# The output projection of a decoder layer by Strassen's scheme, with its operands in the attention's memory

## The chip, the core and the metric

The kernel runs on one core of a Trainium2 chip. A core has TensorE (matrix products; PE in the profile), VectorE (DVE), ScalarE (ACT), GpSimd (POOL) and SyncE (SP, whose queue issues all transfers of this kernel). SBUF is the working memory, PSUM holds eight banks of 512 fp32 columns into which matmuls accumulate. The metric is the device time of one execution in microseconds.

## The reference

```python
h = rmsnorm(x, norm_pre_g)                      # x: (1, 2048, 1024) fp32
z = einsum('bsd,de->bse', h, w_in)              # 1024 -> 4096 columns
q, k, v, g_attn, c_h, c_b, c_c, g_conv = split(z)
# 12 heads of 64, rotary q and k, three dilated windows mixed by their softmax sums
attn_out = o.reshape(B, S, 768) * silu(g_attn)
conv_out = c_b * causal_depthwise_conv(c_c * c_h, conv_w) * silu(g_conv)   # 256 columns
mixed = concatenate([attn_out, conv_out], axis=-1)                         # 1024
y = einsum('bse,ed->bsd', mixed, w_out)         # 1024 x 1024
x = x + rmsnorm(y, norm_post_g)
```

## The kernel before, in words

Precision: an fp32 operand is stored as two parts, a cast to a shorter float (ScalarE) and the rest (VectorE, "split": operand minus cast). A product is three matmuls: high x high, high x low, low x high.

The input projection runs over 32 units of 512 tokens: groups 0 and 7 are the convolution's columns, 1 to 6 pairs of heads, four token chunks each. Normalised x is kept in DRAM as two parts and streamed in by `x_stream` (L472, nine buffers `xp_r`); input weights lie in eight buffers `wp_r`. The four banks of a unit are read by VectorE, for the convolution at L502, L503, L513 and L478. `attn_unit` follows with scores (L627, L655), transposed probabilities (L680), their split (L686) and the products with the values (L699). It keeps keys in `KK`, queries in `q_r` and `q1_r`, values in `v2_r` and `v1_r`, probabilities in `p4_r`, `p1_r` and `pt_r`. Gated results go to DRAM (`mix_d`: L807 from the attention, L523 from the convolution).

The output projection begins when the last product of the attention is done (`gate`). The attention's pool is closed and a new one holds `wo`, the gain `gpost` and other buffers. Sixteen pieces (128 rows x 512 columns) of `w_out` are loaded (L880), cast (L882) and split (L883). For each chunk of 512 tokens eight blocks of the mixed activations are loaded (L892), cast (L893) and split (L894). For each of its four token tiles (128 tokens, every fourth one) and each column half, 8 blocks x 3 matmuls accumulate into one bank (L908 to L910). Then ScalarE squares the bank with a sum over columns (L914), VectorE multiplies it with the gain (L919); the root of the mean square (L921 and the four small operations L382 to L385) scales it onto the residual (L928), and two stores follow (L930).

Order: no engine order is written by hand. Every operation is added to a `Plan` with its engine, an estimated duration, a priority (a lower number goes first) and the buffers that it reads and writes. A list scheduler gives each free engine the ready operation of lowest number; a buffer comes from a `Ring`, whose tokens are handed out in the order in which they were made unless the ring is unordered. The instructions are then issued in that order, and each engine and SP's queue execute theirs in order. URG is a large negative priority for what frees a bank.

Of the kernel before, what the change touches and what calls it, by code (L numbers as in the profile page):

```python
# [34 lines left out]
KT = D // 128  # L35
# [260 lines left out]
def hybrid_layer(ctx: ExitStack, tc: tile.TileContext, x, w_in, w_out, conv_w, g_pre, g_post,  # L296
# [25 lines left out]
    mix_d = [[dram.tile([128, C], F32, name=f"mix{e}_{b}") for b in range(NB)] for e in range(KT)]  # L322
# [26 lines left out]
    attn = ExitStack()  # L349
    ap_ = attn.enter_context(tc.tile_pool(name="attn", bufs=1))  # L350
# [5 lines left out]
    p4_r = ring(ap_, "p4", 2, [128, 4, C])  # L356
    p1_r = ring(ap_, "p1", 2, [128, 4, 256])
# [33 lines left out]
    W = {}  # L391

    def weights_in(grp, i):
# [8 lines left out]
        else:  # L402
# [6 lines left out]
        add("DVE", dvet(C) + 0.07, pc, lambda: vec.tensor_tensor(w.ap[:, 1], raw.ap, f(w.ap[:, 0]), op=ALU.subtract),  # L409
            r=[raw, (w, 0)], w=[(w, 1)], after=XL[i - 1:i] if grp == 0 and i else (), port=True)  # L410
# [58 lines left out]

    def x_stream(n, kt):  # L470
        s = XT[n, kt] = Tok(xp_r)
        add("DMA", dmat(512), n * 100 - 20 + kt, lambda: nc.sync.dma_start(f(s.ap), xt_d[n % NB][kt]), r=[("xt", n % NB, kt)], w=[s])  # L472
# [17 lines left out]
    U = {}  # L490

    def conv_unit(n, i, b, zs):
        pe, pr = URG + n * 100, n * 100 + 60
# [6 lines left out]
        t = table(b, pr - 100) if i else T[b]  # L500
# [22 lines left out]
        add("DMA", dmat(256), pr, lambda: nc.sync.dma_start(mix_d[6 + i][b], g.ap), r=[g], w=[("mix", 6 + i, b)])  # L523
# [5 lines left out]
    def attn_unit(n, p, b, zs):  # L529
# [196 lines left out]
        for i in range(0, len(groups), 2):  # L726
            visit = groups[i:i + 2]
            add("PE", sum(g[0] for g in visit), pr, lambda visit=visit: [g[1]() for g in visit], r=[k for g in visit for k in g[2]],
                w=[k for g in visit for k in g[3]], after=x_last, mode=1)
            for g in visit:  # L730
                g[4]()
# [75 lines left out]
        add("DMA", dmat(256), pr, lambda: nc.sync.dma_start(mix_d[p][b], gs.ap), r=[gs], w=[("mix", p, b)])  # L807

    attn_last = []
# [44 lines left out]
    OUT = {}  # L854
    or_r = uu_r + raw_r + rp_r + g_r

    def open_out():
        if OUT:
            return
        attn.close()  # L860
        op_ = ctx.enter_context(tc.tile_pool(name="outp", bufs=1))
        OUT["wo"] = [op_.tile([128, 2, D], F32R, name=f"wo{e}") for e in range(KT)]
        OUT["gpost"] = op_.tile([128, D], F32, name="gpost")
        for s, t in zip(xr_r, ring(op_, "xr", 2, [128, D])):
            s.ap = t.ap
        for s, t in zip(y_r, ring(op_, "y", 2, [128, D])):
            s.ap = t.ap
        for s, t in zip(mx_r, ring(op_, "mx", 2, [128, 2, C], F32R)):
            s.ap = t.ap
        for s, t in zip(ys_r, ring(op_, "ys", 4, [128, 8])):  # L870
            s.ap = t.ap

    xr_r, y_r, ys_r, mx_r = (Ring([Slot() for _ in range(k)]) for k in (2, 2, 4, 2))
    gate = add("DMA", 0.0, 3300, open_out, after=attn_last, w=["open"])
    add("DMA", dmat(512), 3301, lambda: nc.sync.dma_start(OUT["gpost"], g_post.to_broadcast([128, D])), w=["gpost"], after=[gate])
    for e in range(KT):
        for j in range(2):
            raw = Tok(or_r)
            dl = slice(j * C, (j + 1) * C)
            add("DMA", dmat(256), 3302 + e, lambda e=e, dl=dl, raw=raw: nc.sync.dma_start(raw.ap, w_out[e * 128:(e + 1) * 128, dl]),  # L880
                w=[raw], after=[gate])
            add("ACT", actt(C), 3302 + e, lambda e=e, dl=dl, raw=raw: act.copy(OUT["wo"][e][:, 0, dl], raw.ap), r=[raw], w=[("wo", e, j, 0)])  # L882
            add("DVE", dvet(C), 3302 + e, lambda e=e, dl=dl, raw=raw: vec.tensor_tensor(  # L883
                OUT["wo"][e][:, 1, dl], raw.ap, f(OUT["wo"][e][:, 0, dl]), op=ALU.subtract), r=[raw, ("wo", e, j, 0)], w=[("wo", e, j, 1)], port=True)

    ms_r = mx_r + wp_r
    for b in range(NB):
        MX = []
        for e in range(KT):
            pr = 3320 + 100 * b + e  # L890
            raw, m = Tok(or_r), Tok(ms_r)
            add("DMA", dmat(256), pr, lambda e=e, b=b, raw=raw: nc.sync.dma_start(raw.ap, mix_d[e][b]), r=[("mix", e, b)], w=[raw], after=[gate])  # L892
            add("ACT", actt(C), pr, lambda raw=raw, m=m: act.copy(m.ap[:, 0], raw.ap), r=[raw], w=[(m, 0)])  # L893
            add("DVE", dvet(C), pr, lambda raw=raw, m=m: vec.tensor_tensor(m.ap[:, 1], raw.ap, f(m.ap[:, 0]), op=ALU.subtract),  # L894
                r=[raw, (m, 0)], w=[(m, 1)], port=True)
            MX.append(m)
        for i in range(4):
            pr = 3400 + 100 * b + 20 * i
# [13 lines left out]
            for j in range(2):  # L912
# [3 lines left out]
                if j == 0:  # L916
                    add("DVE", 0.07, pr + URG, lambda sq=sq: vec.tensor_scalar(
                        sq.ap[:, 0:1], sq.ap[:, 4:5], 1.0 / D, EPS, op0=ALU.mult, op1=ALU.add), r=[(sq, 4)], w=[(sq, 0)])
# [58 lines left out]
```

## Time and profile before

| what | value |
|---|---|
| median of 3 runs | 1229.0 us (1225.31 to 1232.68) |
| the profiled execution | 1228.29 us, span of its instructions 1226.5 us |
| TensorE busy | 1213.1 us (99%), 6952 matmuls |
| VectorE busy | 842.0 us (69%) |
| ScalarE busy | 685.6 us (56%) |
| mean granted clock of TensorE | 0.998 |

The span runs from the first to the last instruction; the device time holds some 1.8 us more. Busy time of an engine is the time covered by its instructions; matmuls overlap, and a busy TensorE is not one at its peak. Line numbers are those of the kernel before.

### The profile page before, as it was taken

To read this page: it belongs to the slowest core of one execution; us is meant where nothing else is said; L and a number is where in the kernel's file an instruction comes from. 1 tells how busy PE (TensorE), PEld (TensorE's weight loads), DVE (VectorE), ACT (ScalarE), POOL (GpSimd) and SP (SyncE) were. 2 spreads that over 40 slices of the span, in tenths; PEclk is the share of its full clock that TensorE was granted. 3 is DMA by queue.
4 is the path that set the end of the run, shared out by engine and by line. 5 is a ranking of instruction groups with operands and counts; after the bars stand their busy time and mean duration, and the time that the engine had idled before them with its cause. 6 is when DMAs were issued, how large, how long until landed. Compare 5 with 4: busy or idle time off the path is not lost.

```text
span 1226.5 us, 20984 instructions
## 1 busy us (share of the span) xinstructions
PE 1213.1 (99%) x6952; PEld 1010.5 (82%) x6952; DVE 842.0 (69%) x2179; ACT 685.6 (56%) x1814; POOL 260.6 (21%) x212
## 2 busy tenths in 40 slices
PE   8999999999999999999999999999999999999997
PEld 7888888888878888888888888888888888888886
DVE  5565577877777778786778787787778656544343
ACT  6532546766656667667658666677667434223121
POOL 0011122323222332212323232322333111000000
PEclk9999999999999999999999999999999999999999
DMA  9979677766777666865877757765777759642331
GB/s 344 369 305 343 241 241 258 243 189 211 238 243 224 209 214 219 287 200 160 257 221 268 242 174 268 250 192 189 247 246 270 231 200 374 215 151 94 103 103 69
DMA packets 140573, 279.09 MB, mean 228 GB/s; under 512 B 31536, under 2 KB 73648, under 8 KB 140464
## 3 DMA queue, kind: packets, MB, share of 16 engines
q1 hardware_dynamic: 140464, 277.75, 68.1%
q8 instruction: 55, 0.90, 0.3%
q14 instruction: 54, 0.44, 0.1%
HBM read 214.05 MB, written 51.05 MB: 216 GB/s over the span
## 4 chain that ended last, share of the span: by engine, by line
PE 96%; DVE 1%; DMA 1%; SPq 0%; issue 0%; ACT 0%; DVEq 0%
PE z L844 18%; PE z L846 18%; PE z L845 17%; PE st L699 8%; PE st L680 8%; PE st L909 5%; PE st L908 5%; PE st L910 5%; PE st L627 4%; PE st L655 3%; PE st L844 1%; PE st L846 1%; PE st L845 1%; PE st L441 1%; PE st L590 1%; DMA rp<-rp 0%
## 5 line engine op out<-in xcount | busy, mean ns | idle before, releaser
L844 PE MATMUL z<-xt,w 128*128 128x512 f32 x960 | 397.2, 414 | 0.0
L846 PE MATMUL z<-xt,w 128*128 128x512 f32 x960 | 376.8, 392 | 0.0
L845 PE MATMUL z<-xt,w 128*128 128x512 f32 x960 | 375.4, 391 | 0.0
L846 PEld LDWEIGHTS z<-xt,w 128*128 128x128 f32 x960 | 180.2, 188 | 40.9
L844 PEld LDWEIGHTS z<-xt,w 128*128 128x128 f32 x960 | 180.9, 188 | 32.3 <-issue 3.8
L845 PEld LDWEIGHTS z<-xt,w 128*128 128x128 f32 x960 | 181.3, 189 | 25.8
L686 DVE TENSOR_TENSOR pt<-st,pt 128x512 fp32r<-128x512 f32 x216 | 142.2, 678 | 47.6 <-ACT pt L685 45.7
L638 ACT ACTIVATE p<-p,sm 128x128 f32<-128x128 f32 (+3 forms) x192 | 105.8, 554 | 73.5 <-DVE sm L634 73.1
L685 ACT CAST pt<-st 128x512 fp32r<-128x512 f32 x216 | 119.9, 579 | 36.1 <-PE st L680 34.2
L699 PEld LDWEIGHTS st<-pt,v 128*128 128x128 f32 x852 | 122.1, 190 | 16.8 <-DVE pt L686 4.3
L699 PE MATMUL st<-pt,v 128*128 128x256 f32 x852 | 132.6, 286 | 2.4 <-DVE pt L686 2.4
L680 PE MATMUL st<-cst,p 128*128 128x128 f32 x852 | 121.8, 273 | 0.0
L719 DVE TENSOR_TENSOR uu<-st,uu 64x256 f32<-64x256 f32 x192 | 80.2, 420 | 58.8 <-ACT uu L718 54.8
L748 POOL TENSOR_TENSOR uu<-uu 128x512 f32<-128x512 f32 x48 | 72.4, 1508 | 207.2 <-DVE uu L719 207.1
L680 PEld LDWEIGHTS st<-cst,p 128*128 128x128 f32 x852 | 100.2, 140 | 18.4 <-issue 3.0
L634 DVE CUSTOM_DVE_ANT_0 p<-st,cst 128x128 f32<-128x128 f32 (+3 forms) x192 | 81.8, 487 | 47.5 <-PE st L627 47.2
L717 ACT COPY uu<-st 64x256 f32<-64x256 f32 x192 | 70.2, 368 | 61.9 <-PE st L699 56.0
L666 ACT ACTIVATE p<-p,e 128x256 f32<-128x256 f32 (+1 forms) x192 | 94.7, 498 | 12.2 <-DVE e L662 12.1
L914 ACT ACTIVATE y<-st 128x512 f32<-128x512 f32 x32 | 19.2, 599 | 129.9 <-PE st L910 129.9
L558 POOL TENSOR_TENSOR rp<-rp,cs 128x512 f32<-128x512 f32 x24 | 36.2, 1510 | 228.1 <-DMA rp<-rp 109.0
L662 DVE CUSTOM_DVE_ANT_0 p<-st,cst 128x256 f32<-128x256 f32 (+1 forms) x192 | 66.9, 411 | 21.7 <-PE st L655 21.5
L909 PE MATMUL st<-wo,w 128*128 128x512 f32 x192 | 75.6, 394 | 0.0
(140 smaller groups left out, 1804.6 us busy)
## 6 DMA issues: line engine op xcount, KB each, us to landing
xt<-xt SPq DMA_DIRECT2D x256, 512.0 KB
cs<-t SPq DMA_DIRECT2D x28, 768.0 KB
raw<-in_w_in SPq DMA_DIRECT2D x59, 256.0 KB
rp<-rp SPq DMA_DIRECT2D x192, 64.0 KB
vd<-v SPq DMA_DIRECT2D x96, 128.0 KB
v<-vd SPq DMA_DIRECT2D x24, 512.0 KB
ab<-ad SPq DMA_DIRECT2D x48, 256.0 KB
mix<-g SPq DMA_DIRECT2D x32, 256.0 KB
```

What stands on the lines that cost most here:

```text
L634: add("DVE", dvet(w) + 0.01, pr + URG, lambda h=h, r=r, P4=P4: vec.tensor_tensor_reduce(P4.ap[:, r, 0:w], ps[h].ap[:, (r - r0) * w:(r - r0 ...
L638: add("ACT", actt(w) + 0.19, pr, lambda h=h, r=r, P4=P4: act.activation(P4.ap[:, r, 0:w], P4.ap[:, r, 0:w], AF.Exp, bias=s4(0, h)[:, r:r + ...
L666: add("ACT", actt(256 - lo[g]) + 0.19, pr, lambda h=h, g=g, P1=P1: act.activation(P1.ap[:, g, lo[g]:], P1.ap[:, g, lo[g]:], AF.Exp, bias=E ...
L680: nc.tensor.transpose(ps.ap[:, i * 128:(i + 1) * 128], pp.ap[:, a, c * 128:(c + 1) * 128], ident)
L685: add("ACT", actt(m * 128, True), pr + URG, lambda: act.copy(pt.ap[:, :m, 0, :], p4()), r=[ps], w=[(pt, 0)])
L686: add("DVE", dvet(m * 128), pr + URG, lambda: vec.tensor_tensor(pt.ap[:, :m, 1, :], p4(), f(pt.ap[:, :m, 0, :]), op=ALU.subtract), r=[ps, ...
L699: mm(dst, v, pt.ap[:, i], start=s, stop=e)
L719: add("DVE", dvet(256), pr + URG, lambda: vec.tensor_tensor(cols(a, lo), o()[lo:lo + 64, 0], cols(a, lo), op=ALU.add), r=[O], w=[(a, (h, h ...
L844: mm(z.ap, w.ap[:, 0, js], xt.ap[:, 0], start=kt == 0, stop=False)
L845: mm(z.ap, w.ap[:, 0, js], xt.ap[:, 1], start=False, stop=False)
L846: mm(z.ap, w.ap[:, 1, js], xt.ap[:, 0], start=False, stop=kt == KT - 1)
L909: mm(z.ap, m.ap[:, 0, il], wo[:, 1, dl], start=False, stop=False)
```

## The change

The output projection is done for pairs of token tiles (`q`, eight pairs) as a 2 x 2 block product: rows are the two tiles, the summed index is halved (blocks 0 to 3 and 4 to 7), the columns are the two halves of 512. Winograd's form of Strassen's scheme needs seven block products of 4 blocks x 3 matmuls each: A11 B11, S3 T3, S2 T2, A22 T4, S1 T1, A12 B21, S4 B22, in this order, with four sums of activations (S) and four of weights (T). The sums run on VectorE in fp32 before the cast and split, so there are 28 weight forms (seven for each of four blocks) and seven forms per pair. Three products accumulate onto a bank that already holds another product and has been copied before.

The attention's buffers stay allocated. Weight forms lie in `KK`, the queries', values' and probabilities' buffers; those of `p4_r` and `p1_r` are closed and reopened for six more. Five forms, (B21, 3) and (B22, 0 to 3), lie in input weight buffers and are loaded again (`late`). Token forms use the nine x buffers and three input weight buffers. Two gates open the homes: keys and queries after the last scores, the rest after the last product of the attention. The mixed activations are stored per chunk as (block, row, token) and loaded for four blocks and one tile at a time. Residual loads are halved in size.

```diff
-    mix_d = [[dram.tile([128, C], F32, name=f"mix{e}_{b}") for b in range(NB)] for e in range(KT)]
+    mix_d = [dram.tile([KT, 128, C], F32, name=f"mix{b}") for b in range(NB)]
...
+    FORMS = ("B11", "T3", "T2", "T4", "T1", "B21", "B22")
...
+    wo_r = Ring(early + later + anew[0] + anew[1], False)
+    gates = [gated(early, score_last + w_last, lambda: None), gated(later + anew[0], attn_last + w_last, lambda: layout(0))]
+    home = len(wo_r)
+    ys_r = ring(cp, "ys", 4, [128, 8])
+    wr_r = uu_r + raw_r + list(g_r)[2:]
+    mr_r = uu_r + list(g_r)[2:]
+    or_r = rp_r + g_r
+    wl_r = Ring(list(wp_r)[:4 * len(FORMS) - home], False)
+    ms_r = Ring(list(xp_r) + list(wp_r)[4 * len(FORMS) - home:])
...
+    def part(name, e, t, pr):
+        form = WF[name, e]
+        add("ACT", actt(C), pr, lambda: act.copy(form.ap[:, 0], t.ap), r=[t], w=[(form, 0)])
+        return add("DVE", dvet(C), pr, lambda: vec.tensor_tensor(form.ap[:, 1], t.ap, f(form.ap[:, 0]), op=ALU.subtract),
+                   r=[t, (form, 0)], w=[(form, 1)], port=True)
...
+        def at(name, e=e):
+            return 3303 + 8 * e if e < 2 else 3319 + 2 * FORMS.index(name) + 0.1 * e
...
+        part("B11", e, r11, at("B11"))
+        less("T3", r11, r12, r11)
+        less("T3", r12, r22, r12)
+        part("T3", e, r12, at("T3"))
+        less("T2", r12, r22, r11)
+        part("T2", e, r12, at("T2"))
+        less("T4", r12, r21, r12)
+        part("T4", e, r12, at("T4"))
+        part("T1", e, r11, at("T1"))
...
+        def mixed(half, i):
+            t = Tok(mr_r)
+            x_ops.append(add("DMA", dmat(256), po - 90 + 4 * i + half, lambda b=b, i=2 * h + i: nc.sync.dma_start(
+                cells(t), mix_d[b][4 * half:4 * half + 4, :, 128 * i:128 * i + 128].rearrange("e p t -> p e t")),
+                r=[("mix", 4 * half + k, b) for k in range(4)], w=[t], after=loads[7:8] + streams[-1:]))
+            return t
...
+        a11, a21, a22, a12 = mixed(0, 0), mixed(0, 1), mixed(1, 1), mixed(1, 0)
+        form("A11", a11)
+        sums("S3", a21, a11, a21, ALU.subtract)
+        form("S3", a21)
+        sums("S2", a21, a22, a21, ALU.subtract)
+        form("S2", a21)
+        form("A22", a22)
+        sums("S1", a22, a21, a11, ALU.add)
+        form("S1", a22)
+        form("A12", a12)
+        sums("S4", a12, a12, a21, ALU.subtract)
+        form("S4", a12)
...
+        def keep(bank):
+            y = Tok(or_r)
+            add("ACT", actt(C, True), po + URG, lambda: act.copy(y.ap, bank.ap), r=[bank], w=[y])
+            return y
+        def plus(bank, y):
+            add("DVE", dvet(C), po + URG, lambda: vec.tensor_tensor(y.ap, bank.ap, y.ap, op=ALU.add), r=[bank], w=[y])
...
+        product(0, B[0], "A11", "B11", True)
+        c11 = keep(B[0])
+        product(1, B[1], "S3", "T3", True)
+        c22 = keep(B[1])
+        product(2, B[0], "S2", "T2", False)
+        c21 = keep(B[0])
+        product(3, B[1], "A22", "T4", False)
+        plus(B[1], c21)
+        finish(2 * h + 1, 0, c21, c21, lower)
+        product(4, B[0], "S1", "T1", False)
+        plus(B[0], c22)
+        finish(2 * h + 1, 1, c22, c22, lower)
+        store(2 * h + 1, (c21, c22), lower)
+        product(5, B[2], "A12", "B21", True)
+        plus(B[2], c11)
+        finish(2 * h, 0, c11, c11, upper)
+        product(6, B[0], "S4", "B22", False)
+        c12 = Tok(or_r)
+        finish(2 * h, 1, B[0], c12, upper)
+        store(2 * h, (c11, c12), upper)
```

`product` adds twelve matmuls of 128 x 512 as before; `finish` squares and multiplies with the gain, `store` does the root, the residual and the two stores.

## Rows read from the trace of the kernel before

**Rows 1.** The page: span, busy time of each engine (share of the span, instructions), and the chain of work that ended last.

```profile
span 1226.5 us, 20984 instructions
...
PE 1213.1 (99%) x6952; PEld 1010.5 (82%) x6952; DVE 842.0 (69%) x2179; ACT 685.6 (56%) x1814; POOL 260.6 (21%) x212
...
PE 96%; DVE 1%; DMA 1%; SPq 0%; issue 0%; ACT 0%; DVEq 0%
```

**Rows 2.** The three longest groups of waits of TensorE over the whole span: engine and line that waited, for whom, us in total, times, longest.

```profile
PE st L441 <- DMA p<-in_x: 2.7, 4, 1.1
PE st L699 <- DVE pt L686: 2.4, 1, 2.4
PE st L817 <- DVE u L497: 1.1, 1, 1.1
```

**Rows 3.** The timeline of TensorE around the first and the last matmul of the output projection: start, us of one, engine, line, operation, output<-inputs.

```profile
1041.15 0.39 PE L846 MATMUL st<-xt,w 128*128 128x512 f32 x1
...
1043.87 0.39 PE L846 MATMUL st<-xt,w 128*128 128x512 f32 x1
1044.09 0.39 PE L908 MATMUL st<-wo,mx 128*128 128x512 f32 x1
...
1219.32 0.39 PE L910 MATMUL st<-wo,mx 128*128 128x512 f32 x1
```

**Rows 4.** TensorE's groups of one of the projection's three lines from 1044 us to the end: count, busy us, mean ns of one, idle us before (the other two lines, L908 and L910, have the same two counts).

```profile
L909 PE MATMUL st<-wo,w 128*128 128x512 f32 x192 | 75.6, 394 | 0.0
...
L909 PE MATMUL st<-wo,mx 128*128 128x512 f32 x64 | 24.9, 389 | 0.0
```

**Rows 5.** Busy time of each engine in the stage of the output projection: us and instructions, TensorE's granted clock, DMA share, GB/s.

```profile
1044.09:1219.50 175.41, 175.41 (x769) 144.02 (x767) 77.00 (x188) 42.40 (x104) 2.77 (x2) 1.00 0.37 122
```

**Rows 6.** The timeline of VectorE: the first split of an output weight, neighbouring splits, the last one, the first read of an input projection's bank in the last unit, and the end of the first token tile.

```profile
1007.12 0.68 DVE L883 TENSOR_TENSOR wo<-raw,wo 128x512 fp32r<-128x512 f32 x1
...
1031.31 0.68 DVE L883 TENSOR_TENSOR wo<-rp,wo 128x512 fp32r<-128x512 f32 x1
1031.91 0.68 DVE L883 TENSOR_TENSOR wo<-uu,wo 128x512 fp32r<-128x512 f32 x1
...
1037.33 0.68 DVE L883 TENSOR_TENSOR wo<-rp,wo 128x512 fp32r<-128x512 f32 x1
...
1042.25 0.69 DVE L502 TENSOR_TENSOR rp<-z,cs 128x512 f32<-128x512 f32 x1 [1.84 <-PE z L846]
...
1057.66 0.16 DVE L382 RECIPROCAL ys<-ys 128x1 f32<-128x1 f32 x1 [0.80 <-ACT ys L921]
...
1058.49 1.41 DVE L928 SCALAR_TENSOR_TENSOR y<-y,ys,xr 128x512 f32<-128x512 f32 x2
```

**Rows 7.** VectorE's groups by line and shape from 1044 us to the end.

```profile
L928 DVE SCALAR_TENSOR_TENSOR y<-y,ys,xr 128x512 f32<-128x512 f32 x32 | 22.6, 748 | 0.6
...
L894 DVE TENSOR_TENSOR w<-uu,w 128x512 fp32r<-128x512 f32 x7 | 5.7, 842 | 0.0
...
L894 DVE TENSOR_TENSOR w<-g,w 128x512 fp32r<-128x512 f32 x4 | 2.7, 688 | 0.0
```

**Rows 8.** ScalarE's groups from 1044 us to the end.

```profile
L914 ACT ACTIVATE y<-st 128x512 f32<-128x512 f32 x32 | 19.2, 599 | 129.9 <-PE st L910 129.9
L914 ACT ACTIVATION_READ_ACCUMULATOR y<-st 128x1 f32 x32 | 6.2, 194 | 0.0
L921 ACT ACTIVATE ys<-ys 128x1 f32<-128x1 f32 x16 | 4.7, 295 | 0.5
...
L893 ACT CAST w<-g 128x512 fp32r<-128x512 f32 x4 | 2.5, 621 | 0.2
```

**Rows 9.** The timeline of the tail, all engines.

```profile
1219.75 0.60 ACT L914 ACTIVATE y<-st 128x512 f32<-128x512 f32 x1 [4.79 <-PE st L910]
...
1222.80 0.99 SPq L930 DMA_DIRECT2D out<-y  x2
```

**Rows 10.** The timeline at the kernel's start: a split on VectorE and the matmul that waits for it.

```profile
10.25 0.68 DVE L409 TENSOR_TENSOR w<-raw,w 128x512 fp32r<-128x512 f32 x1
...
10.97 0.47 PE L844 MATMUL z<-xt,w 128*128 128x512 f32 x1
```

**Rows 11.** The timeline of TensorE: the last scores and the last attention product.

```profile
985.49 1.71 PE L655 MATMUL st<-kk,q 64*128 64x256 f32 x24
...
1000.07 0.63 PE L699 MATMUL st<-pt,v 128*128 128x256 f32 x4
```

**Rows 12.** The timeline of SP's DMA queue: the first and the last load of an output weight.

```profile
1001.11 0.43 SPq L880 DMA_DIRECT2D raw<-in_w_out  x1
...
1031.66 0.45 SPq L880 DMA_DIRECT2D rp<-in_w_out  x1
```

**Rows 13.** Busy time of each engine from 985 to 1053 us, columns as in rows 5; the last line is the sum over six stretches.

```profile
1021.00:1031.00 10.00, 10.00 (x46) 8.29 (x45) 8.33 (x14) 5.90 (x10) 4.23 (x3) 1.00 1.04 406
...
sum 68.00, PE 68.00 PEld 56.52 DVE 46.43 ACT 29.03 POOL 13.25; mean PE 11.33 PEld 9.42 DVE 7.74 ACT 4.84 POOL 2.21
```

**Rows 14.** The same columns at the kernel's start and behind the last matmul.

```profile
5.00:10.00 5.00, 2.62 (x16) 1.94 (x16) 2.44 (x4) 2.93 (x6) 0.00 (x0) 1.00 0.93 285
...
1219.00:1227.00 8.00, 0.71 (x4) 0.25 (x2) 2.82 (x8) 0.98 (x3) 0.00 (x0) 0.82 0.17 66
```

More of the change, by code (lines that the diff above doesn't have):

```diff
@@ L408, in weights_in @@
         add("ACT", actt(C), pc, lambda: act.copy(w.ap[:, 0], raw.ap), r=[raw], w=[(w, 0)])
[L409 to L410 removed]
+        w_last[:] = [add("DVE", dvet(C) + 0.07, pc, lambda: vec.tensor_tensor(w.ap[:, 1], raw.ap, f(w.ap[:, 0]), op=ALU.subtract),
+                         r=[raw, (w, 0)], w=[(w, 1)], after=XL[i - 1:i] if grp == 0 and i else (), port=True)]
     XT, XL, x_last = {}, [], []
@@ L873, in hybrid_layer @@
[L873 to L878, printed above, removed]
-            dl = slice(j * C, (j + 1) * C)
[L880 to L884, printed above, removed]
@@ new lines, in hybrid_layer @@
+    FORMS = ("B11", "T3", "T2", "T4", "T1", "B21", "B22")
+    WF = {}
+    flat = [t.rearrange("p a b -> p (a b)") for t in KK] + [r[0].ap.rearrange("p a b -> p (a b)") for r in (q_r, q1_r)]
+    rest = [s.ap.rearrange("p a b c -> p (a b c)") for s in v2_r + pt_r] + [s.ap.rearrange("p a b -> p (a b)") for s in v1_r]
+    early, later = ([Slot(t[:, i:i + 2 * C].rearrange("p (a b) -> p a b", a=2)) for t in ts for i in range(0, t.shape[1], 2 * C)]
+                    for ts in (flat, rest))
+    anew = [[Slot() for _ in range(n)] for n in (4, 2)]
@@ new lines, in layout, with gated @@
+    def layout(i, **kw):
+        old[i].close()
+        p = ctx.enter_context(tc.tile_pool(name=f"wo{i}", bufs=1, **kw))
+        for k, s in enumerate(anew[i]):
+            s.ap = p.tile([128, 2, C], F32R, name=f"wo{i}{k}")
+    def gated(slots, done, fn):
+        held = [Tok(Ring([s])) for s in slots]
+        add("DMA", 0.0, -2e6, lambda: None, w=held)
+        return add("DMA", 0.0, 3300, fn, r=held, after=done)
+    wo_r = Ring(early + later + anew[0] + anew[1], False)
+    gates = [gated(early, score_last + w_last, lambda: None), gated(later + anew[0], attn_last + w_last, lambda: layout(0))]
@@ new lines, in hybrid_layer, with post @@
+    home = len(wo_r)
[5 more added lines that the diff above has]
+    ms_r = Ring(list(xp_r) + list(wp_r)[4 * len(FORMS) - home:])
+    gpost, junk2 = Tok(ab_r), Tok(u_r)
+    def post(j):
+        return gpost.ap.rearrange("p a b c -> p (a b c)")[:, j * C:(j + 1) * C]
+    add("DMA", dmat(512), 3301, lambda: nc.sync.dma_start(gpost.ap.rearrange("p a b c -> p (a b c)"), g_post.to_broadcast([128, D])), w=[gpost], after=gates[1:])
@@ new lines, in combine, with fetch @@
+    def combine(prio, w, o, a, b, op, ro, ra, eng="DVE"):
+        add(eng, dvet(w) if eng == "DVE" else poolt(w), prio,
+            lambda: (vec if eng == "DVE" else pool).tensor_tensor(o(), a(), b(), op=op), r=ra, w=[ro], port=True)
+    for name in FORMS:
+        for e in range(4):
+            k = FORMS.index(name) * 4 + e
+            WF[name, e] = Tok(wo_r if k < home else wl_r)
+    loads = []
+    def fetch(e, h, j, prio, after, ring_=None):
+        t = Tok(ring_ or wr_r)
+        loads.append(add("DMA", dmat(256), prio, lambda: nc.sync.dma_start(
+            t.ap, w_out[(4 * h + e) * 128:(4 * h + e + 1) * 128, j * C:(j + 1) * C]), w=[t], after=after))
+        return t
```

161 lines of the change are left out of this document (88 added, 73 removed).

## Prediction

> **What bounds the kernel now.** I read the page first: its span, its engine shares and the chain that ended last. TensorE is busy 99% of 1226.5 us and is 96% of the chain; VectorE has 69% and ScalarE 56% [rows 1]. Next I asked which waits of TensorE the profile finds at all: the three longest groups are 3.8 us at the kernel's start (transfers, a cleared buffer) and 2.4 us once in the attention [rows 2]. So the time is the number of matmuls times their pace, and a change that removes matmuls is worth its full price as long as nobody lets TensorE wait. Then I went to the stage that is changed. The timeline shows its first matmul (L908) at 1044.09, directly behind the last matmul of the input projection (L846, 1043.87), and its last (L910) at 1219.32 [rows 3]. The groups by line count 192 + 64 on each of the three lines [rows 4], 768 matmuls. From first start to last start are 767 steps: (1219.32 - 1044.09) / 767 = 0.2285 us each; the listed 0.39 us is a duration with the next matmul already inside it and is of no use as a price. The stage table shows why room is left for other engines: in these 175.4 us VectorE is busy 77.0 and ScalarE 42.4 us, the DMA engines 37% [rows 5].
>
> **What is removed.** Per pair of token tiles (128 tokens each) the old stage makes 2 tiles x 2 column halves x 8 row blocks x 3 = 96 matmuls; the new one makes 7 products x 4 x 3 = 84 of the same shape, and there are 8 pairs. So 768 - 672 = 96 fall away: 96 x 0.2285 = **21.9 us**. The matmuls that stay load as many weights and stream as many columns, so I keep their pace. If products switch a little slower than the old groups, the nearest row is the input projection, where twelve steps take the 2.72 us from 1041.15 to 1043.87 [rows 3], 0.2267 each: no loss from that side.
>
> **What is added to VectorE in the steady stage.** Its durations need the same care. Splits next to each other stand 0.60 us apart while each is listed at 0.68 [rows 6], so the price lies between 0.60 (start to start) and 0.688 (duration [rows 7]). Per pair there are now 7 splits of a token form, 4 sums, 3 additions from a PSUM bank, and, as before, 4 products with the norm's gain: 18 operations of 512 columns. The four final multiply-adds take 1.41 us for two [rows 6], the small ones of one token tile 0.83 from L382 to L928 [rows 6], and an estimated 0.2 for L917 and L923, one column wide like L382 (0.16). Low end: 18 x 0.60 + 2 x 1.41 + 2 x 1.03 = 15.7 us; high end, by durations: 18 x 0.688 + 4 x 0.748 + 2 x 1.03 = 17.4 us. TensorE needs 84 x 0.2285 = 19.2 us for the pair. VectorE goes from 77.0 / 175.4 = 44% to 82 or 91%, and stays under the bound. [...] I take the low end, since it is what back-to-back splits show. POOL, whose work stretched single splits to 0.84 on average [rows 7], has two operations in the whole stage [rows 5], the last of the convolution.
>
> **ScalarE** gets 7 casts at 0.62 us, 3 copies out of PSUM priced like a square at 0.60, 4 squares at 0.60 + 0.19 and 2 roots at 0.30 [rows 8]: 4.3 + 1.8 + 3.2 + 0.6 = 9.9 of 19.2 us. Hidden.
>
> **Banks that are read between products.** Product 2 adds into the bank that ScalarE copies after product 0; products 3, 4 and 6 do the same after 1, 2 and 4. Between them lies one other product, 12 x 0.2285 = 2.74 us. The hand-over: from the last matmul's start to ScalarE's read 0.43 us (1219.32 to 1219.75), the read 0.60 [rows 3, 9], and back to TensorE 0.04, as the trace's only clear case shows (a split from 10.25 for 0.68, the matmul waiting for it at 10.97 [rows 10]): 1.1 us. That is covered with 1.6 us to spare, if the reader's own queue isn't blocked. Behind each of these reads stand casts and splits of the next pair in the same in-order queue, so a late one delays both. The last of them (product 6) waits for VectorE, the fuller engine. Bounds per pair: 0 and one blocked operation with its partner, about 1.3 us. I take 0.3 x 8 = **2.4 us**.
>
> **The tail** stays: last matmul, square, root, four small ones, two multiply-adds, two stores: 1219.32 to 1226.5 [rows 1, 3, 9]. VectorE has 4.8 us of bank work in the last two products' 5.5 us, so it may arrive up to 1 us late. I add **0.5 us**.
>
> **The start of the stage** is where the change asks most. 28 weight forms for 16 pieces mean 28 casts, and 28 splits plus 16 subtractions on VectorE, against 16 and 16. The loads can begin earlier: the homes in the keys' and queries' memory open when the last scores are done (987.2) instead of the last attention product (1000.7) [rows 11], and loads that started at 1001.11 ended in a last split at 1037.33 [rows 6, 12]. From 985 to 1053 VectorE is busy 46.4 us [rows 13], of which 16 + 4 + 6 splits for this stage are about 19.0 us (26 x 0.688, and an estimated 1.1 more for those that POOL held up). 68 - (46.4 - 19.0) = 40.6 us are left. The new demand by 1053 is 44 x 0.60 + 11 x 0.60 (forms of the first pair) = 33 us. Some 4 us of the room lie before the first loads land. So it fits with 3 to 4 us to spare if gaps could be used fully; five forms (the ones that wait for the input projection's weight buffers) aren't needed before the sixth and seventh product, 13.7 us after the stage starts. In the bad case the preparation runs as it did: 16 splits from 1007.12 to 1037.33, 1.9 us each [rows 6]; 39 operations from 990 on then end at 1064, with the fifth product due at 1044.1 + 11.0 = 1055: 9 us of stall. VectorE also reads the input projection's banks just in time here (L502 starts at 1042.25 while the unit's matmuls run until 1043.87 [rows 3, 6]), so one foreign operation in front of each of the two remaining changes of unit costs up to 0.6 us. Bounds: 0 and 10 us. I take **2.5 us**, nearer to the low end, as the order is made by a planner whose 0.6 us for a split is the distance that the trace shows.
>
> **Transfers.** The mixed activations now come in runs of 512 bytes instead of 2 KB, still 256 KB a load and 4 loads a pair. The stage moved bytes at up to 406 GB/s when the DMA engines were full [rows 13], so 256 KB take at least 0.65 us; at a quarter of that speed (each packet costing as much as now) 2.6 us. With 2 MB for residual and output (5.2 us) that makes 7.8 to 15.6 of 19.2 us per pair, and the loads run a pair ahead. Nothing on the path; were the cover gone, one late load would cost about its own 2.6 us. The extra 1.3 MB for the forms that are fetched late take 3.2 us of DMA time, behind the saturated stretch [rows 13]. SP has 12 issues a pair at about 0.4 us; behind a blocked one stand the next pair's loads, with most of a pair of slack.
>
> **Sum.** 1228.3 (the profiled execution, span plus 1.8) - 21.9 + 2.4 + 0.5 + 2.5 = 1211.8. The median of the three runs is 1229.0, so both give the same; I say **1211.5 us**.
>
> **Rivals.**
> *The start is late.* The first pair's forms or weights come 8 to 16 us behind. For it: VectorE's spare room is a few us, and buffers for raw pieces are shared between weights and mixed activations. Against: 36 us from first load to last split were enough for 16 pieces without one wait of TensorE. Time: 1206.4 + 8 to 16 + 2 = 1216 to 1224.
> *VectorE is the bound of the steady stage.* Its 34 operations a pair at their durations with 0.1 us of waiting each make 17.4 + 3.4 = 20.8 us, 1.6 over TensorE's 19.2. In place of the 2.4 us for the banks that is 8 x 1.6 = 12.8: 1209.4 + 12.8 = 1222. For it: 82 to 91% leave little. Against: the distances of 0.60 [rows 6].
> *Slower.* The place is the bank shared by two products with one between them. It decides when the hand-over lasts 2.74 + 21.9 / 32 = 3.4 us in all 32 cases; at 4 us it gives 32 x 1.26 = 40 us and 1247. For it: the reader's queue is in order and 82% full. Against: 1.1 us without queueing.
> [...]
> *Nothing happens* to the count can't be: 96 matmuls are not issued.
>
> **How the numbers follow.** Full gain with under 8 us of stalls, 1204 to 1214.5: 0.62. Late start: 0.17. VectorE's bound: 0.09. Gain eaten up (clock, or most of several of these): 0.06. Slower by the banks: 0.06. No stall gives 1206.4, and runs differ by 0.3% either way, which sets the low end at 1204; the high end 1222 takes in most of the first two rivals. Two versions of this kernel can be told apart from about 0.5%, 6 us. Below 1222.9 lie the first case (0.62), most of the late start (0.14) and of VectorE's bound (0.07), together 0.83; from there to 1235 the rest of these and most of the eaten gain, 0.10; above, 0.07.
>
> **What would show it.** TensorE's groups of the projection: 672 matmuls at 0.2285 us. The stage from first to last matmul: 153.5 us plus some 5 us of waits; waits on VectorE's splits in the first pair, or on its additions before product 6. VectorE at 80 to 90% in the middle of the stage. The granted clock at 1.00. I am wrong if the first product starts well after 1047, if the waits of TensorE exceed 10 us, or if the matmuls before 1040 moved.

## The result and the profile after

The changed kernel takes 1219.5 us (median of 6, 1215.9 to 1222.9) against 1228.9 of the kernel before: ratio 0.9923, interval 0.9897 to 0.9949. So it is faster by some 9 us; the forecast was 1211.5 us with a range of 1204 to 1222. Line numbers from here on are those of the changed kernel: L1008 to L1010 are the three matmuls of a product's row block, L976 casts a token form and L977 splits it, L898 is every sum of two pieces, L914 and L915 cast and split a weight form, L1015 copies a bank and L1019 adds to it, L848 to L850 are the input projection and L524 is the last POOL operation of a convolution unit.

The page of the changed kernel: span, busy time, chain that ended last (rows of before: [rows 1]). The profiled execution, 1222.9 us, is the slowest of the six.

```profile
span 1220.8 us, 20955 instructions
...
PE 1201.8 (98%) x6856; PEld 993.4 (81%) x6856; DVE 916.0 (75%) x2287; ACT 717.9 (59%) x1874; POOL 260.1 (21%) x212
...
PE 84%; DVE 8%; DMA 3%; ACT 2%; issue 1%; SPq 1%; DVEq 0%; ACTq 0%
```

TensorE has the 96 matmuls less (6952 to 6856), and VectorE now holds 8% of the chain where it had 1%. The longest waits of TensorE after ([rows 2]):

```profile
PE st L442 <- DMA p<-in_x: 3.2, 4, 1.7
PE st L703 <- DVE pt L690: 1.9, 1, 1.9
PE st L1008 <- ACT xt L976: 1.8, 1, 1.8
```

The third is new and lies in the changed stage. TensorE's timeline there, around the first product, the wait, one steady pair of token tiles (84 matmuls, from 1116.12 to 1135.63) and the end ([rows 3]):

```profile
1051.26 0.39 PE L850 MATMUL st<-xt,w 128*128 128x512 f32 x1
1051.49 0.39 PE L1008 MATMUL st<-kk,xt 128*128 128x512 f32 x1
...
1057.36 0.40 PE L1010 MATMUL st<-wo,xt 128*128 128x512 f32 x1
1059.54 0.50 PE L1008 MATMUL st<-v,xt 128*128 128x512 f32 x1 [1.79 <-ACT xt L976]
...
1116.12 0.39 PE L1008 MATMUL st<-kk,w 128*128 128x512 f32 x1
...
1135.63 0.39 PE L1008 MATMUL z<-kk,xt 128*128 128x512 f32 x1
...
1213.46 0.39 PE L1010 MATMUL st<-w,xt 128*128 128x512 f32 x1
```

Three things are to be read here. The first product follows the input projection by 0.23 us, as before, but at 1051.49 instead of 1044.09: 7.4 us were lost ahead of the stage. The stage lasts 161.97 us from first to last matmul, where 671 x 0.2285 = 153.3 were expected without waits. And a steady pair takes 19.51 us without one gap, which is 84 x 0.2323: not a pause here and there but a slower step at every matmul. Read off at every 84th matmul, the eight pairs take 23.80, 20.45, 20.38, 19.51, 19.52, 19.51, 19.51 and (83 steps) 19.29 us. So stalls of 4.3, 0.9 and 0.9 us lie in the first three pairs, 6.1 together, and none behind them.

Busy time of the engines after, in stretches from the preparation to the steady stage; columns as in [rows 5]:

```profile
1020.00:1040.00 20.00, 20.00 (x90) 16.57 (x89) 19.52 (x29) 6.59 (x11) 5.88 (x4) 1.00 0.94 326
1040.00:1060.00 20.00, 18.17 (x78) 13.96 (x76) 19.04 (x31) 8.45 (x16) 2.95 (x2) 1.00 0.49 160
...
1060.00:1065.00 5.00, 5.00 (x16) 3.78 (x15) 4.25 (x8) 2.82 (x7) 0.00 (x0) 0.66 0.36 128
...
1120.00:1160.00 40.00, 40.00 (x174) 32.28 (x173) 32.68 (x71) 17.66 (x40) 0.00 (x0) 1.00 0.48 159
```

VectorE is busy 19.5 of 20 us while the weight forms are made and 82% in the steady stage. The granted clock is 1.00 except behind the wait: 0.66 from 1060 to 1065, where six steps in a row, from 1060.86 to 1063.42, took 0.43 us each instead of 0.23, nearly twice as long; from 1061 to 1063 the granted clock reads 0.50. The wait itself, in three engines' timelines:

```profile
1056.63 1.66 POOL L524 TENSOR_TENSOR rp<-rp,rp 128x512 f32<-128x512 f32 x1 [3.55 <-DVE rp L522]
1057.07 1.77 DVE L898 TENSOR_TENSOR uu<-uu 128x512 f32<-128x512 f32 x1
1058.87 1.14 ACT L976 CAST xt<-uu 128x512 fp32r<-128x512 f32 x2 [3.31 <-DVE uu L898]
...
1061.45 0.69 DVE L898 TENSOR_TENSOR uu<-uu 128x512 f32<-128x512 f32 x1
```

The sum for the third product took 1.77 us instead of 0.69. It began while POOL's operation ran, until 1058.29, and the cast and TensorE waited for it. The sum ended 0.55 us after POOL's operation, near the 0.60 us by which unhindered neighbours stand apart in [rows 6], as if it had begun only when POOL was done; why the two do not run side by side was not shown.

### The profile page after: what moved, and what is told of

Same layout as the page of the kernel before. It is cut to its first block, busy times and chain, and to the rows that moved or that the text cites. A ratio compares the mean times of both kernels' runs of the same rounds, so it can differ in the third digit from the quotient of the medians.

```text
span 1220.8 us, 20955 instructions
## 1 busy us (share of the span) xinstructions
PE 1201.8 (98%) x6856; PEld 993.4 (81%) x6856; DVE 916.0 (75%) x2287; ACT 717.9 (59%) x1874; POOL 260.1 (21%) x212
## 4 chain that ended last, share of the span: by engine, by line
PE 84%; DVE 8%; DMA 3%; ACT 2%; issue 1%; SPq 1%; DVEq 0%; ACTq 0%
PE z L848 16%; PE z L850 16%; PE z L849 16%; PE st L703 8%; PE st L684 7%; PE st L631 4%; PE st L659 3%; PE st L1010 2%; PE st L1008 2%; PE st L1009 2%; DMA rp<-rp 1%; PE z L1008 1%; PE z L1010 1%; PE z L1009 1%; ACT p L642 1%
## 5 line engine op out<-in xcount | busy, mean ns | idle before, releaser
L848 PE MATMUL z<-xt,w 128*128 128x512 f32 x960 | 397.1, 414 | 0.0
L850 PE MATMUL z<-xt,w 128*128 128x512 f32 x960 | 377.7, 393 | 0.0
L850 PEld LDWEIGHTS z<-xt,w 128*128 128x128 f32 x960 | 180.5, 188 | 40.3
L848 PEld LDWEIGHTS z<-xt,w 128*128 128x128 f32 x960 | 181.2, 189 | 32.7 <-issue 3.4
L721 ACT COPY uu<-st 64x256 f32<-64x256 f32 x192 | 70.2, 368 | 58.7 <-PE st L703 52.3
L562 DVE TENSOR_TENSOR rp<-rp,cs 128x512 f32<-128x512 f32 x72 | 55.9, 791 | 23.4 <-DMA rp<-rp 23.0
L722 ACT COPY uu<-st 64x256 f32<-64x256 f32 x192 | 69.6, 367 | 3.2 <-DVE uu L723 0.4
```

What stands on the lines that cost most here:

```text
L562: add(e, dur, pr, lambda o=o, a=a, i=i, eng=eng: eng.tensor_tensor(o.ap, a.ap, cs.ap[:, i], op=ALU.mult), r=[cs], w=[o], port=True)
L848: mm(z.ap, w.ap[:, 0, js], xt.ap[:, 0], start=kt == 0, stop=False)
L850: mm(z.ap, w.ap[:, 1, js], xt.ap[:, 0], start=False, stop=kt == KT - 1)
```

## The experiments

**Is the loss ahead of the stage the same each time?** The changed kernel unedited:

> The changed kernel unedited. In the first profile the projection began 7.4 us later than before, although every instruction up to there is issued in the same order on every engine. Theory U1 (transfers land a little earlier or later from run to run): the start of the first projection matmul scatters between 1043 and 1052 us, the stage itself stays at 162 us, and the median over all runs is 1216 to 1221. Theory U2 (the new places of the attention's buffers slow it down): the start is at 1050 to 1052 again and so is every later profile of a kernel with this layout.

Measured: 1218.05 us, ratio 0.9921 (0.9903 to 0.9938). TensorE's first and last matmul of the stage, and the clock behind the wait:

```profile
1046.54 0.39 PE L1008 MATMUL st<-kk,xt 128*128 128x512 f32 x1
...
1208.11 0.39 PE L1010 MATMUL st<-w,xt 128*128 128x512 f32 x1
```

```profile
1060.00:1065.00 5.00, 5.00 (x24) 4.01 (x23) 4.06 (x8) 2.83 (x6) 0.00 (x0) 1.00 0.64 195
```

The stage repeats (161.57 us, stalls of 5.7, steady pairs of 19.51); what lies ahead of it does not, by 5 us. Behind the second product TensorE waits as long as in the first profile (1.95 us more than a step in both), yet the clock stays at 1.00, so the some 1.5 us that the low clock cost in the first profile are not part of the wait's price. Over both sets, 12 executions, the median is 1218.8.

**The start of the stage.** Two versions: one leaves out the 16 weight sums, the other loads three raw pieces of the first block and makes the first pair's token sums early.

```
notsum
         def less(name, o, a, b):
-            combine(at(name), C, lambda: o.ap, lambda: a.ap, lambda: b.ap, ALU.subtract, o, [k for k in (a, b) if k is not o])
+            pass
q0first
-    late = []
+    late, first0 = [], Ring(list(raw_r))
...
-        r11, r12, r22, r21 = (fetch(e, h, j, 3303 + 8 * e, gates[e == 1:][:1], first_r if e == 1 else None) for h, j in ((0, 0), (0, 1), (1, 1), (1, 0)))
+        r11, r12, r22, r21 = (fetch(e, h, j, 3303 + 8 * e, gates[1:] if e == 1 else w_last if not e and (h, j) != (1, 0) else gates[:1], first_r if e == 1 else first0 if not e and (h, j) != (1, 0) else None) for h, j in ((0, 0), (0, 1), (1, 1), (1, 0)))
...
-            m, pr = M[name], po - 80 + 4 * order.index(name)
+            m, pr = M[name], (po - 80 if q else 3300) + 4 * order.index(name)
...
```

> The sixteen subtractions that form the weight sums are left out (the forms are cast and split from the raw pieces, so the products are not those of the scheme). Theory A (VectorE cannot prepare forms in time at the start of the stage): 9.6 us of its work are gone, the first pair takes 19.5 to 20.5 us instead of 23.8, the granted clock stays at 1.00, and the whole is 4 to 6 us faster than the changed kernel. Rival B (the hand-over of banks between products stalls TensorE): the stage stays within 1 us.

> Three of the first block's four raw weight pieces are loaded before the keys' memory is free, and the forms of the first token pair go ahead of the weight forms. Theory A: first pair 20.5 to 22 us instead of 23.8, later pairs a little longer since the same work is due later, 1 to 3 us faster in all. Rival B: no change. Rival D (a matter of total work and not of order): the first pair gains what the second loses, within 0.5 us in all.

Measured: 1215.32 us (0.9874 to 0.9912) and 1216.73 us (0.9889 to 0.9924). Without the sums the first pair takes 19.51 us, the second 21.13 and the stage 157.45; the whole is 3.5 us below the changed kernel, a little less than the 4 to 6 expected. The stretches of this version, and an operation of POOL and one of VectorE:

```profile
1020.00:1040.00 20.00, 20.00 (x90) 16.57 (x89) 17.21 (x25) 6.22 (x11) 5.90 (x4) 1.00 1.01 339
1040.00:1060.00 20.00, 20.00 (x89) 16.20 (x88) 16.12 (x26) 9.25 (x18) 2.98 (x2) 1.00 0.47 152
```

```profile
1050.61 1.67 POOL L524 TENSOR_TENSOR rp<-rp,rp 128x512 f32<-128x512 f32 x1 [3.55 <-DVE rp L522]
1051.05 1.79 DVE L977 TENSOR_TENSOR xt<-g,xt 128x512 fp32r<-128x512 f32 x1
```

An operation beside POOL's takes just as long here, 1.79 us, and TensorE doesn't wait: VectorE at 17.2 and 16.1 instead of 19.5 and 19.0 of 20 us has a lead to lose. The kernel before has such an operation too (L894 at 1049.78 us, 1.79 us, beside POOL's L520 from 1049.34 to 1051.02) and no wait. So such an operation alone does not stall the first pair; VectorE's lack of room does, and POOL's operation marks where it breaks. How much of the wait would be left without POOL's operation was not tested. With the early pieces the first pair takes 19.53 us too, but the second 22.73, with a wait for a split of 1.7 us (stage 159.08): part of the lateness went on to the next pair.

Seven buffers for raw token pieces instead of five, taken from the residual's six:

```
-    mr_r = uu_r + list(g_r)[2:]
+    mr_r = uu_r + list(g_r)[2:] + list(raw_r)[1:]
-    xr_r = Ring(tables + list(raw_r))
+    xr_r = Ring(tables + list(raw_r)[:1])
```

> The changed kernel with seven buffers for raw token pieces instead of five: two of the three that held residual pieces. Theory (the stalls of the first three pairs come from VectorE's capacity between 1007 and 1065 us): about 5 us of stalls stay, in the first pair, and the stage takes 160 to 162 us. Rival (the stalls come from buffers that come free late): they fall under 2 us and the stage takes under 158 us. If both hold together, the first pair keeps its stall and the second and third lose theirs (0.9 us each).

Measured: 1217.69 us (0.9883 to 0.9929), stage 160.56; the first three pairs take 23.91, 19.81 and 19.51 us. The first keeps its stall (and in this execution, too, the clock fell behind it: 0.77 from 1060 to 1065), the second's falls to 0.3 us and the third's is gone. More buffers do not help the first pair, then. For the next two they are not the only remedy: without the sums and with the early pieces the third pair takes 19.51 us as well, with five buffers. And one profile of each is a thin basis, as the second pair's stall was 0.9 us in the first profile of the changed kernel and 2.0 in the next. What shares room and buffers have in these two stalls stays open.

**The slower step.** A kernel of nothing but these matmuls, with operand tiles at seven places in SBUF, each pair of tiles for 36 matmuls:

```
    grid = [(i, j) for i in range(7) for j in range(7)]
...
                nc.tensor.matmul(o, m[:, 0, el], w[:, 0], start=r == 0 and e == 0, stop=False)
                nc.tensor.matmul(o, m[:, 0, el], w[:, 1], start=False, stop=False)
                nc.tensor.matmul(o, m[:, 1, el], w[:, 0], start=False, stop=r == 2 and e == 3)
```

> Nothing of the layer is computed: only matmuls in the kernel's pattern (high by high, high by low, low by high, 512 columns), 36 for each of 49 pairs of a stationary and a moving tile, at seven places of the memory, with no other engine at work. Three tiles lie low (below 103,000 bytes), four high (from 139,000), two of them shifted by 320 and one by 448 bytes against the others modulo 4096. Theory P1 (the pace depends on where the two operands lie): pairs differ, 0.227 us a matmul for some and 0.229 to 0.233 for others; by halves if low with high is slow, by offset if a shift of 320 or 448 is slow. Rival P2 (other engines' traffic slows TensorE): all 49 pairs at 0.227 us or less.

Measured, over 34 steps from the second matmul of a pair to its last, us per step; rows: the stationary tile (the matmul's operand of 128 columns), columns: the moving one (512 columns); in brackets the tile's start past a multiple of 4096 bytes. The times are read to 0.01 us, so a cell is good to 0.0003; "start" is the kernel's first pair, whose first steps took 0.43 us:

```
            ta     tb     tc     tg     td     te     tf
ta (128)  start  .2268  .2291  .2279  .2268  .2291  .2332
tb (128)  .2276  .2265  .2291  .2279  .2268  .2291  .2332
tc (448)  .2332  .2332  .2274  .2332  .2332  .2274  .2332
tg (128)  .2279  .2268  .2291  .2279  .2268  .2291  .2332
td (128)  .2276  .2265  .2291  .2279  .2268  .2291  .2332
te (448)  .2332  .2332  .2274  .2332  .2332  .2274  .2332
tf (576)  .2291  .2288  .2324  .2291  .2288  .2324  .2267
```

Two of the cells in TensorE's timeline (out<-moving,stationary), second and last matmul of each:

```profile
71.92 0.39 PE L329 MATMUL z<-tb 128*128 128x512 f32 x1
...
79.62 0.39 PE L330 MATMUL z<-tb 128*128 128x512 f32 x1
...
121.35 0.39 PE L329 MATMUL z<-ta,tc 128*128 128x512 f32 x1
...
129.28 0.39 PE L330 MATMUL z<-ta,tc 128*128 128x512 f32 x1
```

7.70 against 7.93 us for 34 steps. What decides is how the two operands lie to each other: at equal places 0.2265 to 0.2279, with the stationary one 320 bytes further 0.2332, with the moving one 320 bytes further 0.2291. Which half of the memory a tile is in makes no such difference; why two of the four moving tiles that lie level take 0.2278 and two 0.2267 is open. Within a tile the stationary operand moves by 512 bytes from one row block to the next, and level pairs keep their step at all of them, so what counts is the place past a multiple of 512 at most; a smaller period was not looked for. In the changed kernel the tokens start 3776 bytes past a multiple of 4096 and most weight forms 3456, just these 320 bytes; the forms in the input weights' buffers lie level with the tokens. Its trace has both steps side by side: from the fourth pair on 0.228 us behind a matmul with a form in those buffers and 0.233 behind all others, 0.2323 as a mean. Before, the weights and two of ten token buffers lay level and eight stood 448 bytes apart: hence 0.2285, a mix of 0.2267 and 0.2289.

Two kernels move their buffers by padding alone:

```
align (changed kernel)
+    ap_.tile([128, 80], F32, name="pad")
     KK = [ap_.tile([128, 4, NB * 128], F32R, name=f"kk{i}") for i in range(2)]
...
+    ctx.enter_context(tc.tile_pool(name="padr", bufs=1, side="right")).tile([128, 72], F32, name="padr0")
basealign (kernel before)
+        op_.tile([128, 112], F32, name="pad")
         OUT["wo"] = [op_.tile([128, 2, D], F32R, name=f"wo{e}") for e in range(KT)]
```

> The changed kernel with 320 bytes of padding in front of the attention's memory and 288 bytes behind it, so that the weight forms (which lay 3456 and 4064 bytes past a multiple of 4096) lie 3776 bytes past one, as the token forms do; nothing else. Theory (pace by the two operands' places): every pair of tiles from the third on takes 84 x 0.2267 = 19.05 us instead of 19.51 us; the stage takes 671 x 0.2267 + 5.7 us of stalls = 157.8 us instead of 161.6; the median falls by about 3.7 us, to 1214.4. Rival (the slower pace is the hand-over of the banks, the 2.4 us of the prediction spread thin): the pairs stay at 19.51 us and the time does not move. The attention's probabilities move too, so the matmuls that transpose them (L684) may change their own pace, 0.0900 us in the median before the change and 0.0950 after; neither theory says which way.

> The kernel before with 448 bytes of padding in front of the output stage's memory, so that its weights, which lay 448 bytes beside eight of the ten token buffers (by their place past a multiple of 4096), lie level with them. Theory (pace by places): the projection's step falls from 0.2285 to 0.2267 us, the stage from 175.2 to 173.9 us, the time by 1.4 us, about as much as three rounds can tell. Rival: the step stays at 0.2285. It is also a second look at the matmuls ahead of the projection, which its edit does not touch: if the first projection matmul starts near 1044 us again, the later start in the changed kernel (1046.5 and 1051.5 us) is the changed kernel's own; if it starts 2 to 7 us later, it is scatter between executions.

Measured: 1217.39 us (0.9888 to 0.9923) and 1228.13 us (0.9975 to 1.0002). A steady pair of the first, and first and last matmul of the second:

```profile
1110.20 0.39 PE L1010 MATMUL st<-kk,w 128*128 128x512 f32 x1
...
1129.24 0.39 PE L1010 MATMUL z<-kk,xt 128*128 128x512 f32 x1
```

```profile
1048.57 0.39 PE L909 MATMUL st<-wo,mx 128*128 128x512 f32 x1
...
1222.42 0.39 PE L911 MATMUL st<-wo,mx 128*128 128x512 f32 x1
```

19.04 us are 84 x 0.2267, and 173.85 / 767 = 0.2267. Both kernels take the level step when their operands are level, and the rival (banks) falls. The stage of the first shrinks by less than its eight pairs give (8 x 0.47 = 3.8): it takes 159.12 us, as its stalls in the first three pairs grew to 7.0. The medians move the right way but can't be told from those of the unpadded kernels: what is shown is the step and the stage, not the whole time.

**Where 3 us ahead of the stage went.** Take the median, less the 1.8 or 2.1 us around the span, less the tail, less the stage: the projection starts at 1229.0 - 1.8 - 7.2 - 175.2 = 1044.8 before and at 1218.8 - 2.1 - 7.3 - 161.8 = 1047.6 after. Single traces can't show these 2.8 us: basealign, whose work ahead of the stage is that of the kernel before, started it at 1048.57, the kernel before at 1044.09. The instructions ahead of the first loads are the same in the same order on each engine, so two sets of places that differ were given to the kernel before, each by itself.

```
basemix
-    mix_d = [[dram.tile([128, C], F32, name=f"mix{e}_{b}") for b in range(NB)] for e in range(KT)]
+    mix_d = [dram.tile([KT, 128, C], F32, name=f"mix{b}") for b in range(NB)]
...
baseplace
+    ap_.tile([128, 32], F32, name="pad0")
...
+    pt_r = ring(ap_, "pt", 3, [128, 4, 2, 128], F32R)
     p4_r = ring(ap_, "p4", 2, [128, 4, C])
+    ap_.tile([128, 152], F32, name="pad1")
     p1_r = ring(ap_, "p1", 2, [128, 4, 256])
-    pt_r = ring(ap_, "pt", 3, [128, 4, 2, 128], F32R)
```

> The question is where some 3 us went ahead of the projection: the changed kernel's stage is 13.5 us shorter, its median 10.2 us lower, while every engine's order of work up to the projection's first loads is the same. This is the kernel before with one part of the change alone: the mixed activations lie in four DRAM tensors of 2 MB instead of 32 of 256 KB, as in the changed kernel; each is still written and read in the same runs. If DRAM places cost the 3 us: the median rises from 1229 to 1232 and the first projection matmul starts some 3 us after 1044 to 1048. If not: 1229 within 1.5 us.

> The kernel before with another part of the change alone: the attention's buffers lie in SBUF where the changed kernel has them (the whole block 128 bytes further up, the transposed probabilities in front of the probabilities, the second set of probabilities at 221152). If these places cost the 3 us ahead of the projection (the matmuls that transpose probabilities took 0.0950 us in the median in the changed kernel and 0.0900 before): the median rises to 1232 and the groups of L680 and L699 together take 187.5 to 189 us instead of 185.2. If not: 1229 within 1.5 us.

Measured: basemix 1231.85 us, ratio 1.0026 (1.0016 to 1.0036), which is 2.0 to 4.4 us slower; its stage takes 175.23 us as before, so the loss lies ahead of it. Its trace does not show where: the execution that was profiled, 1229.87 us, is the fastest of twelve and started the projection at 1045.67. baseplace 1230.12 us, 1.0012 (1.0000 to 1.0024), not told from nothing. Its groups L680 and L699 take 187.0 us together (from start to next start), but in basealign, with the old places, they take 187.5: that sign told nothing. Nor did the matmuls that transpose probabilities change their pace: within a group the next starts after 0.109 us in the median in the kernel before, in baseplace and in the changed kernel, not after 0.0900 and 0.0950. So the way the mixed activations lie in DRAM, and with them all DRAM tensors allocated after them, is enough for the 3 us; that the attention's places add something is not excluded. By what path it slows the kernel stays open. The loss is no accident of one version: by the same sum as above, the six other versions of the changed kernel that keep these four tensors start the projection at 1047.7 to 1049.1.

**The parts together.** First all three edits (places, early pieces, seven raw buffers), then without the last:

> Three edits together: operands at equal places, the first weight pieces loaded and the first pair's token sums made before the attention ends, and two more buffers for raw token pieces. Theory (pace, and a start limited by both VectorE's room and buffers): pairs at 19.05 us, under 2 us of stalls, the stage 671 x 0.2267 + 1.5 = 153.6 us, 8 us shorter than in the changed kernel, and a median of about 1210. If the pace is not set by the places: 157.4 us and 1213.7. If the start's stalls do not depend on buffers: 155.3 us and 1211.7.

> The changed kernel with operands at equal places and with the first weight pieces and the first token sums made early, but with the buffers for raw token pieces and residual pieces as the change has them (five and six). In the version with three edits two waits for the reading of a bank came up in the fourth and sixth pair (0.63 and 0.42 us), with residual buffers cut from six to four. If that cut made them: no waits from the third pair on, pairs of 19.04 us, and 3.2 us of stalls in the second pair as without the placing: stage 671 x 0.2267 + 3.2 = 155.3 us. If a faster TensorE alone brings them: waits for banks here as well, and a stage of 156 us or more.

Measured: 1214.92 us (0.9863 to 0.9901) and 1214.93 us (0.9861 to 0.9897); stages of 155.97 and 156.17 us, so the first missed the 153.6 and 1210 expected of it. TensorE's waits on the two, first with seven raw buffers, then with five:

```profile
PE st L1011 <- DVE wo L917: 0.7, 1, 0.7
...
PE st L1010 <- ACT rp L1017: 0.7, 1, 0.7
...
PE st L1010 <- DVE rp L1021: 0.5, 1, 0.5
```

```profile
PE st L1012 <- DVE w L979: 1.7, 1, 1.7
...
PE z L1010 <- ACT xt L978: 0.4, 1, 0.4
PE st L1010 <- ACT w L978: 0.3, 1, 0.3
```

(Two lines of padding put L1017 and L1021 where L1015 and L1019 were.) In the version with seven raw buffers, and so four for the residual, products wait for the copy of a bank and for an addition to it, the waits that the prediction priced. With five and six they are gone even at the faster step: pairs of 19.04 us from the third on. The same exchange of buffers made no such wait at the slower step (19.51 us from the third pair on, above), so the waits need both, and whether the four or the seven buffers make them was not told apart. The exchange also lengthens the tail, from 7.3 to 8.4 us. Without it the second pair keeps 4.1 us of stalls, so the two come out equal.

Last, the mixed activations in eight DRAM tensors of 1 MB:

```
-    mix_d = [dram.tile([KT, 128, C], F32, name=f"mix{b}") for b in range(NB)]
+    mix_d = [[dram.tile([4, 128, C], F32, name=f"mix{h}_{b}") for b in range(NB)] for h in range(2)]
```

> The version with equal places and the early first weights and sums, with one thing changed: the mixed activations in eight DRAM tensors of 1 MB (one for each half of the row blocks) instead of four of 2 MB; the same instructions, and the allocator gives the other DRAM tensors other places. If the 3 us that the four tensors of 2 MB cost the kernel before come from where things lie in DRAM, this moves the start of the projection by some us one way or the other (best case: back by 3 us, to a median of 1212). If not, 1214.9 again within 1.5 us. The stage itself stays at 156 us either way.

Measured: 1213.17 us, ratio 0.9872 (0.9856 to 0.9889), stage 156.15. It is the fastest version, 15.2 us below the kernel before, but its lead of 1.8 us on the one without this edit is not resolved.

## Why the prediction was partly right

The direction held; the number was 6.6 to 8 us too low, within the range. But the time lies above the 1204 to 1214.5 us of the likeliest case, though that case's condition, under 8 us of stalls, was met. It lies in the 1216 to 1224 us of the late start, which is not how it came about. The range held because it had been widened for rivals that did not happen; that part is luck. From 1229.0 to 1218.8 the terms, as the traces give them, are -21.9 (96 matmuls at 0.2285), +2.5 (671 steps of 0.2323 instead of 0.2285), +5.9 (stalls, mean of two profiles), +0.1 (tail), +0.3 (around the span) and, as the remainder, +2.9 ahead of the stage (2.8 by the sum above; the difference is rounding). Step by step:

- **What bounds the kernel**: right. TensorE's steps and waits account for the whole stage.
- **What is removed**: the count was right, the step failed at "so I keep their pace". The matmuls have the same shape but other operands' places. The sign stood in [rows 4], where one of two groups of the same shape lasts 394 and the other 389 ns, and in the 0.2267 of the input projection, which I took as "no loss from that side" when it was the better of two paces. Cost: 2.5 us. Measured by placing (pace, align, basealign).
- **VectorE in the steady stage**: right at the low end taken, 82%; the rival of a VectorE bound did not come about.
- **ScalarE** and **transfers**: hidden, as said (ScalarE 44%, DMA 48% of the steady stretch).
- **Banks**: 2.4 us taken, none measured. The lower bound was the right one, and the upper kind of wait exists: it came at the faster step with buffers moved from the residual to the raw pieces, 0.63 and 0.42 us over the step.
- **The tail**: 0.5 taken, 0.1 measured (from 7.2 to 7.3 us).
- **The start**: the mechanism was right (VectorE's room, the waits in the first pairs), the term too small: 2.5 us taken, 5.7 and 6.1 measured. Room counted over the whole 68 us was "3 to 4 us to spare"; in the last 40 us, around the first wait, VectorE had hardly any (busy 19.5 and 19.0 of 20 us), and the first pair's forms come last. The lower clock for a moment added some 1.5 us in one profile and nothing in the other.
- **Ahead of the stage**: not in the sum at all. "If the matmuls before 1040 moved" was named as a sign of error, and they did: by 2.8 us at the median. So was a first product "well after 1047": it started at 1051.49 in one profile and at 1046.54 in the other. The kernel before with the new DRAM tensors alone loses 3.0 us (2.0 to 4.4).

The terms for banks, tail and start add up to 5.4 us where 6.0 were measured: there the errors cancelled. What missed is the pace and the stretch ahead, 5.3 us together, both from where things lie and neither from the arithmetic. Another 1.0 us was given away in the sum: taken from the median of 1229.0 it gives 1212.5, not the 1211.5 that was said. The rival "the start is late" is not what happened, though the first product began at 1051.5: it stood 0.23 us behind the input projection's last matmul. Nor did the clock eat up the gain: beyond that moment, it was granted at 1.00. What a fall costs stood in the kernel before. Behind the longest wait of [rows 2], in the attention, it has a stretch with a granted clock of 0.50, and in it matmuls of 128x512:

```profile
364.00:367.00 3.00, 2.74 (x10) 2.45 (x11) 2.98 (x18) 2.37 (x9) 2.25 (x2) 0.50 0.77 310
```

```profile
364.26 1.65 PE L699 MATMUL st<-pt,v 128*128 128x256 f32 x6 [2.40 <-DVE pt L686]
365.71 0.63 PE L844 MATMUL z<-xt,w 128*128 128x512 f32 x1
366.14 0.63 PE L845 MATMUL z<-xt,w 128*128 128x512 f32 x1
366.57 0.63 PE L846 MATMUL z<-xt,w 128*128 128x512 f32 x1
```

They start 0.43 us apart where the projection's start 0.23 apart. So a single wait of 2.4 us can be followed by a fall, and the price, nearly twice the step, could have been read there.

## What to carry to other kernels

Moving an operand into another buffer is a change to each matmul that reads it (here the places alone moved the step between 0.2265 and 0.2332 us): compare the step (start to start over many) of groups of one shape, look for two values, and place operands level before counting on the faster one. Spare room of an engine must be counted in the stretch that ends with the first consumer, not over the whole preparation. When a change also regroups DRAM tensors, time that regrouping in the kernel before by itself; a part that alters no order can cost 3 of the 13 us that the stage gained.

## What was not expected of the hardware

- The step of a 128x128 by 128x512 matmul in three passes ran from 0.2265 to 0.2332 us with nothing changed but the places of its two operands; the slow value belongs to the stationary one lying 320 bytes further, the moving one lying 448 bytes further, or 128 bytes between them (0.2324 to 0.2332).
- Four DRAM tensors of 2 MB for 32 of 256 KB, read and written in the same runs, cost the kernel before 3.0 us (2.0 to 4.4) ahead of the stage that reads them.
- In the changed stage a wait of 1.95 us and one of 1.97 us left the granted clock at 1.00 (the changed kernel's second profile, and with equal places), while one of 1.95 and one of 2.45 us were followed by 0.66 and 0.77 over 5 us. The wait in the attention near 364 us tells the same: 1.2, 1.4 and 2.1 us left it at 1.00 in three traces, 1.6 to 2.4 us were followed by a stretch of slower steps in ten (granted clock 0.50 and steps of 0.43 us in the kernel before and in the changed one). The length of the wait alone does not decide; what does is open.
